# A decoder layer with expert retrieval: split weights in the first pass, selection in halves, w_o by blocks, plain fp32 for every other first-table tile

## The chip, the cores and the metric

One core of a Trainium2 chip. The metric is device time in microseconds for one execution of the program. The engines named below are TensorE (PE; its weight loads are PEld), VectorE (DVE), ScalarE (ACT), GpSimd (POOL, which issues the indirect gathers) and SyncE (SP, which issues nearly all other DMAs).

## The reference, cut to what matters

512 tokens, width 1024, all float32. One layer and a final norm:

```python
xn = rmsnorm(h, ln_mix_g)
q, k, v, pz, ga, gp = split(xn @ w_in + b_in)        # 30 column blocks of 128
y_a = sliding_window_attention(q, k, v, sinks) @ w_attn_up
y_p = multiscale_pool(pz, w_pool_grp, pool_scale) @ w_pool_up
h = h + (sigmoid(ga) * y_a + sigmoid(gp) * y_p) @ w_o
xn = rmsnorm(h, ln_ffn_g)
# retrieval: 8 heads, two halves of 128 keys each
sc = einsum(xn @ w_query, sub_keys)                  # 16 column blocks of 128
sv, si = top_k(sc, 16)                               # per token, head and half
fv, fi = top_k(all pairs of sv, 16); idx = pairs of si at fi   # 128 experts of 16384 per token
a = gelu(sum(u_tab[idx] * xn)); g = softmax(fv)      # per token and chosen expert
h = h + sum((g * a) * v_tab[idx])
out = rmsnorm(h, ln_final_g)
```

## The kernel before

**Tokens.** Four blocks of 128 tokens. The mixing runs in two passes of two blocks (`mixing`, L179): blocks 0 and 1 (GB, CB), then blocks 2 and 3. The retrieval is done in two ways. Blocks 2 and 3 go through the whole expert tables as matrix products ("dense"). Block 0 fetches its 128 u rows and 128 v rows per token by indirect DMA. Block 1 fetches its u rows only, and takes part in the dense product with the v table. One gathered row tile (128 tokens by 1024, 512 KB) with the DVE operation on it is called a unit: 128 dots for block 1, 128 dots and 128 additions for block 0, so 384 units in all.

**Products.** fp32 operands go to PE as they are (`mm`, L198, two instructions for each product). Split operands (`mm3`, L112) are high and low parts in the fp32r type, three instructions for each product; the high part is an ACT cast (L124), the low part a DVE subtraction (L119).

**A pass.** Normalise and transpose the inputs (`xT`), project k and v (z 8, 9), then q (z 0 to 7) with attention woven in, then four pooling columns (z 10 to 13), sixteen gate columns (z 14 to 29), the two up projections (L276), w_o for both blocks together (L293, eight weight tiles), residual and second norm, the turn of the normed rows into `qx` (L311), then the sixteen w_query columns with the match against the sub keys (`match`, L322) and the top 16 of each (`top16`, L479). All projections of both passes are plain fp32. A weight tile is 512 KB, in one of four raw buffers (`raw`, L130). The second pass is a generator that starts (inputs, k and v) before the first pass's w_query (`hooks[2]`).

**Selection.** `select` (L492) turns the top 16 of all heads of a block into 128 expert numbers (`ei`) and weights (`gw`), all on DVE but one exponential.

**Background work.** `feed` (L169) takes work from a list: selection of block 1, 40 dots of block 1, selection of block 0, the other 88 dots, then block 0's dots and additions. `tick` (L175) spends a given cost from that list at points of the second pass; what it traces is ordered behind the last "paced" instruction, but only on that instruction's engine. In most of the pass that is ACT, so DVE and POOL work may be issued earlier; in the up projections and in w_o it is a DVE instruction (L288). Within the mixing and table stages a greedy scheduler orders each engine's instructions by readiness and program order.

**First table stage** (`run`, L760). For each of the 128 u tiles, `part` loads it, splits it and makes 24 split products for blocks 2 and 3 (`u_part`, L605); the gelu goes to a held tile or to DRAM (`ahead`). Beside each tile 3.4 cost units of selection (blocks 2 and 3) and of one-hot work are spent (`onehot`, L548: three times, ACT makes 5 of 8 matrices in the first two), and 0.9 units of gathered rows.

**Dense stage** (`dense`, L684). Written out by hand: for each of the 128 v tiles a weight `mix`, the split of the v tile, 18 products of 128 x 512, and an equal share of the units that are left.

Of the kernel before, what the change touches and what calls it, by code (L numbers as in the profile page):

```python
# [11 lines left out]
F32 = mybir.dt.float32  # L12
# [7 lines left out]
P = 128  # L20
# [43 lines left out]
class Layer:  # L64
# [69 lines left out]

    def norm(self, x, g, out):
# [43 lines left out]
    def mixing(self, mp, b0, xn2, hooks):  # L179
# [4 lines left out]
        xT = self.m.tile([P, KD, TU], F32, name="xT", tag="xT", bufs=2)  # L184
# [15 lines left out]
        def z(f, dst, w=None):  # L200
            ps = self.mm_tile(TU)
            mm(ps, w or self.raw(a["w_in"][f]), xT)
# [8 lines left out]
        w89 = [None, None]  # L211
        if first:
            w89 = [self.raw(a["w_in"][f]) for f in (8, 9)]
            hooks[0]()
        for x, r in zip(xs, rows):
            n = t4()
            self.norm(x, self.gm, n)
            self.across(n, lambda ps, r=r: nc.scalar.copy(xT[:, :, r], ps))
        kz, vT = t2()[:, :TU], t2()[:, :TU]
        z(8, kz, w89[0])  # L220
# [4 lines left out]
        z(9, vT, w89[1])  # L225
# [50 lines left out]
        for h in range(4):  # L276
# [12 lines left out]
            tick(2.5 * T_O)  # L289
# [3 lines left out]
        ps = [self.big([P, 2, 512], "ho") for _ in bs]  # L293
        for k in range(KD):
            w = self.raw(a["w_o"][k])
            for j, r in enumerate(rows):
                for n in range(2):
                    nc.tensor.matmul(ps[j][:, n, :], lhsT=mT[:, k, r], rhs=w[:, n * 512:(n + 1) * 512],
                                     start=k == 0, stop=k == KD - 1)
            tick(T_W)  # L300
        hooks[2]()
        qx = self.m.tile([P, KD, TU], F32, name="xT", tag="xT", bufs=2)
        for j, b in enumerate(bs):
# [3 lines left out]
            nc.vector.tensor_tensor(hb, ps[j].rearrange("p a b -> p (a b)"), hb, op=ALU.add)  # L307
            if b != GB:
                nc.sync.dma_start(out=self.hspill[b - CB], in_=hb)
            nat = self.nat[b] if first else t4()  # L310
            self.norm(hb, self.gf, nat)  # L311
            puts = [lambda ps, r=rows[j]: nc.scalar.copy(qx[:, :, r], ps)]  # L312
            if not first:
                puts.append(lambda ps, r=rows[j]: self.low(ps, xn2[0][:, :, r], xn2[1][:, :, r]))
                puts.insert(1, lambda ps, r=rows[j]: nc.scalar.copy(xn2[0][:, :, r], ps))
            self.across(nat, *puts)
# [5 lines left out]
        def match(i, qT):  # L322
# [6 lines left out]
            for j, b in enumerate(bs):  # L329
# [6 lines left out]
        for i in range(16):  # L336
            w = self.raw(a["w_query"][i])
            ps = self.mm_tile(TU)
            mm(ps, w, qx)
# [5 lines left out]
            tick(T_S)  # L345
        match(i, last)

    def mixed(self, xn2):
        nc, a, tc = self.nc, self.a, self.tc
        with tc.tile_pool(name="merged", bufs=1) as self.m, ExitStack() as ps, tc.tile_pool(name="mixing", bufs=1) as mp:  # L350
# [14 lines left out]
            two = self.mixing(mp, HALF, xn2, (nothing, nothing, nothing))  # L365
            one = self.mixing(mp, 0, None, (rest, self.consts, lambda: next(two)))
            for _ in one:
                pass

            def room():  # L370
                t = mp.tile([P, 2048], F32, name="sk", tag="sk", bufs=1)
# [19 lines left out]
            def picked(b):  # L391
                yield from self.select(room(), eq, self.sv[b], self.si[b], self.ei[b], self.gw[b])
# [7 lines left out]
            assert self.work[2].done  # L400
# [91 lines left out]
    def select(self, t, wide, sv, si, ei, g):  # L492
# [3 lines left out]
        v.tensor_copy(sf, si)  # L496
        svp = sv.rearrange("p (h t) k -> p h t k", t=2)
        sfp = sf.rearrange("p (h t) k -> p h t k", t=2)
        v.tensor_scalar(sfp[:, :, 0, :], sfp[:, :, 0, :], float(NKEY), None, op0=ALU.mult)
        cv, ce = t("cv", [P, PH, NCAND]), t("ce", [P, PH, NCAND])  # L500
        for src, dst in ((svp, cv), (sfp, ce)):
            for a0, na, n, off in SEGS:
                v.tensor_tensor(dst[:, :, off:off + na * n].rearrange("p h (a b) -> p h a b", a=na),
                                src[:, :, 0, a0:a0 + na].unsqueeze(3).to_broadcast([P, PH, na, n]),
                                src[:, :, 1, :n].unsqueeze(2).to_broadcast([P, PH, na, n]), op=ALU.add)
        fv, fi = t("fv", [P, PH, TOPK]), t("fi", [P, PH, TOPK], U32)
        yield 5 * SC
        for n in range(0, PH, 4):
# [4 lines left out]
        v.tensor_copy(ff, fi)  # L513
        g = g.rearrange("p (h k) -> p h k", h=PH)
        v.tensor_tensor(g, fv, fv[:, :, 0:1].to_broadcast([P, PH, TOPK]), op=ALU.subtract)
        few = t("few", [P, PH, NFEW])
        for a0, na, n, off, at in FEW:
            v.tensor_copy(few[:, :, at:at + na * n], ce[:, :, off:off + na * n])
        for k0, k1, nh, pos, cand in ((0, 8, 4, self.fewpos, few), (8, 16, 2, self.iota[:, :NCAND], ce)):
            nk, w = k1 - k0, cand.shape[2]  # L520
            for h in range(0, PH, nh):
                if k0 == 8 and h == 0:
                    nc.scalar.activation(g, g, AF.Exp)
# [7 lines left out]
        v.tensor_copy(ei, ef.rearrange("p h k -> p (h k)"))  # L531
        den = t("gden", [P, PH])
        v.reduce_sum(den, g, axis=AX.X)
        v.reciprocal(den, den)
        v.tensor_tensor(g, g, den.unsqueeze(2).to_broadcast([P, PH, TOPK]), op=ALU.mult)
# [69 lines left out]
    def u_part(self, n, w, xn2):  # L605
# [290 lines left out]
```

## Time and profile before

| what | us |
|---|---|
| three runs | 1760.51, 1753.23, 1763.14 (median 1760.51) |
| profiled execution | 1754.47 |
| its span | 1752.7 |
| first pass, up to its last w_query column | about 0 to 303 |
| second pass, up to its last match | about 303 to 640 |
| first table stage | about 640 to 1166 |
| dense stage and end | about 1166 to 1753 |

Over the span PE is busy 1572.9 us (90%), DVE 1275.5 (73%), ACT 726.9 (41%), POOL 535.3 (31%); 486.34 MB are moved, 277 GB/s in the mean. A share of the whole span says little here, since the stages have different limits; the rows below are by stage. A matmul's duration is not its cost: products are pipelined, and the cost is the distance from one start to the next.

### The profile page before, as it was taken

To read this page: it belongs to the slowest core of one execution; us is meant where nothing else is said; L and a number is where in the kernel's file an instruction comes from. 1 tells how busy PE (TensorE), PEld (TensorE's weight loads), DVE (VectorE), ACT (ScalarE), POOL (GpSimd) and SP (SyncE) were. 2 spreads that over 40 slices of the span, in tenths; PEclk is the share of its full clock that TensorE was granted. 3 is DMA by queue.
4 is the path that set the end of the run, shared out by engine and by line. 5 is a ranking of instruction groups with operands and counts; after the bars stand their busy time and mean duration, and the time that the engine had idled before them with its cause. 6 is when DMAs were issued, how large, how long until landed. Compare 5 with 4: busy or idle time off the path is not lost.

```text
span 1752.7 us, 24708 instructions
## 1 busy us (share of the span) xinstructions
PE 1572.9 (90%) x8701; PEld 1346.2 (77%) x8701; DVE 1275.5 (73%) x2797; ACT 726.9 (41%) x1391; POOL 535.3 (31%) x390
## 2 busy tenths in 40 slices
PE   6999999578995978889999999989999999998997
PEld 5788678456872868878888999978778777777876
DVE  2520126898067579997787899759989888888988
ACT  3531021242201124479999766433333333333334
POOL 0000000056007202343222233325555555454551
PEclk9999999798997989989999999999999999999999
DMA  5344443179549637679999999998999999999995
GB/s 175 114 154 152 156 139 133 40 286 363 195 161 383 228 126 248 245 266 327 314 333 317 326 351 350 367 300 317 362 357 389 381 371 351 378 369 375 375 340 185
DMA packets 188027, 486.34 MB, mean 277 GB/s; under 512 B 17024, under 2 KB 82560, under 8 KB 184576
## 3 DMA queue, kind: packets, MB, share of 16 engines
q1 hardware_dynamic: 131392, 279.75, 45.6%
q0 software_dynamic: 55296, 201.35, 31.5%
q10 hardware_dynamic: 1216, 3.67, 0.6%
q8 instruction: 68, 1.11, 0.3%
q14 instruction: 55, 0.45, 0.1%
HBM read 447.35 MB, written 36.83 MB: 276 GB/s over the span
## 4 chain that ended last, share of the span: by engine, by line
PE 31%; ACT 10%; DMA 8%; DVE 6%; issue 3%; SPq 0%; DVEq 0%; ACTq 0%
DMA wr<-v_experts 7%; PE acc L115 6%; PE acc L116 6%; PE acc L114 6%; PE mm L114 4%; PE mm L116 3%; PE mm L115 3%; DVE wl L119 3%; ACT wh L124 3%; ACT gs L589 2%; PE pg L588 2%; ACT ohj L576 2%; ACT ohj L567 2%; DVE row L707 1%; DMA gar<-ahead 1%
## 5 line engine op out<-in xcount | busy, mean ns | idle before, releaser
L701 POOL DMA_INDIRECT row<-u_experts,ei x256 | 342.6, 1338 | 944.4 <-DVE row L707 406.0
L119 DVE TENSOR_TENSOR wl<-wr,wh 128x1024 fp32r<-128x1024 f32 x256 | 311.5, 1219 | 88.6 <-ACT wh L124 87.6
L124 ACT CAST wh<-wr 128x1024 fp32r<-128x1024 f32 x256 | 268.2, 1049 | 184.7 <-PE mm L115 120.6
L198 PE MATMUL mm<-xT,wr 128*128 128x256 f32 x1472 | 337.1, 387 | 3.3 <-ACT xT L312 2.2
L115 PE MATMUL acc<-wl,wh 128*128 128x512 f32 x768 | 305.9, 398 | 20.3 <-DVE wl L119 20.2
L114 PE MATMUL mm<-xh,wh 128*128 128x256 f32 x1024 | 296.2, 291 | 28.6 <-ACT gk L618 12.7
L707 DVE SCALAR_TENSOR_TENSOR row<-row,nat 128x1024 f32<-128x1024 f32 x256 | 309.6, 1217 | 15.4 <-DMA row<-u_experts,ei 15.0
L198 PEld LDWEIGHTS mm<-xT,wr 128*128 128x128 f32 x1472 | 282.1, 194 | 45.9 <-issue 3.4
L114 PE MATMUL acc<-wh 128*128 128x512 f32 x768 | 303.5, 395 | 14.7 <-ACT wh L124 7.7
L116 PE MATMUL acc<-wh,wl 128*128 128x512 f32 x768 | 302.5, 394 | 0.0
L116 PE MATMUL mm<-xh,wl 128*128 128x256 f32 x1024 | 288.4, 285 | 15.6 <-DVE wl L119 15.0
L115 PE MATMUL mm<-xl,wh 128*128 128x256 f32 x1024 | 288.7, 283 | 0.0
L701 POOL DMA_INDIRECT row<-v_experts,ei x128 | 192.0, 1500 | 235.2 <-DVE hg L730 180.0
L114 PEld LDWEIGHTS mm<-xh,wh 128*128 128x128 f32 x1024 | 193.8, 190 | 37.0 <-ACT gk L618 16.1
L116 PEld LDWEIGHTS mm<-xh,wl 128*128 128x128 f32 x1024 | 193.1, 190 | 19.1 <-DVE wl L119 19.1
L115 PEld LDWEIGHTS mm<-xl,wh 128*128 128x128 f32 x1024 | 194.4, 190 | 0.0
L115 PEld LDWEIGHTS acc<-wl,wh 128*128 128x128 f32 x768 | 146.3, 191 | 60.8 <-DVE wl L119 30.9
L114 PEld LDWEIGHTS acc<-wh 128*128 128x128 f32 x768 | 146.3, 191 | 50.2 <-ACT wh L124 11.4
L116 PEld LDWEIGHTS acc<-wh,wl 128*128 128x128 f32 x768 | 146.4, 191 | 29.7
L730 DVE SCALAR_TENSOR_TENSOR hg<-row,act,hg 128x1024 f32<-128x1024 f32 x128 | 163.6, 1278 | 0.5
L656 ACT CAST wh<-gt 128x128 fp32r<-128x128 f32 x128 | 38.1, 298 | 282.8 <-PE acc L115 236.6
L588 PE MATMUL pg<-ohi,ohj 128*128 128x128 f32 x768 | 103.0, 285 | 7.0 <-ACT ohj L576 6.6
(185 smaller groups left out, 1627.5 us busy)
## 6 DMA issues: line engine op xcount, KB each, us to landing
wr<-u_blocks SPq DMA_DIRECT2D x128, 512.0 KB
wr<-v_experts SPq DMA_DIRECT2D x128, 512.0 KB
wr<-w_in SPq DMA_DIRECT2D x60, 512.0 KB
spill<-gs SPq DMA_DIRECT2D x24, 1024.0 KB
gt<-spill SPq DMA_DIRECT2D x64, 384.0 KB
wr<-w_query SPq DMA_DIRECT2D x32, 512.0 KB
wr<-w_attn_up SPq DMA_DIRECT2D x16, 512.0 KB
wr<-w_o SPq DMA_DIRECT2D x16, 512.0 KB
```

Of the source, the lines that this page charges most:

```text
L114: mm(out, lhsT=l[0], rhs=r[0], start=first, stop=False)
L115: mm(out, lhsT=l[0], rhs=r[1], start=False, stop=False)
L116: mm(out, lhsT=l[1], rhs=r[0], start=False, stop=last)
L119: self.lowered = self.nc.vector.tensor_tensor(lo, src, hi.bitcast(F32), op=ALU.subtract).ins
L124: self.nc.scalar.copy(hi, raw)
L198: nc.tensor.matmul(ps, lhsT=w[:, k * P:(k + 1) * P], rhs=x[:, k, :], start=k == 0, stop=k == nk - 1)
L567: nc.scalar.activation(ohj[:, z, :], self.iota, AF.Abs, bias=tr[:, 1, u + z:u + z + 1])
L588: nc.tensor.matmul(pg[:, z, :], lhsT=ohj[:, z, :], rhs=ohi[:, z, :], start=True, stop=True)
L656: nc.scalar.copy(h1, g1)
L701: self.nc.gpsimd.indirect_dma_start(out=t, out_offset=None, in_=tab, in_offset=bass.IndirectOffsetOnAxis(ap=ei[:, s:s + 1], axis=0))
L707: self.nc.vector.scalar_tensor_tensor(u, u, 1.0, self.nat[b], op0=ALU.mult, op1=ALU.mult, accum_out=self.act[b][:, s:s + 1])
L730: nc.vector.scalar_tensor_tensor(z, v, self.act[GB][:, s:s + 1], z, op0=ALU.mult, op1=ALU.add)
```

## The change

1. **First pass in split products.** `plan` and `fetch` load, cast and subtract each w_in and w_query tile of the first pass, one tile ahead; high and low parts lie in the six row buffers that the gathers use later. `xh`, `xl` take the place of `xT` and `qx` there. The second pass stays plain fp32.
2. **w_o one block at a time**: eight weight tiles for block 0, residual and norm, the same eight again for block 1 (16 loads a pass). Then `turn(0)`, the start of the next pass, in the second pass the first halves of three w_query columns (`FILL`), `turn(1)`.
3. **Selection by halves of the heads.** Heads 0 to 3 of block 1 are selected inside the first pass's w_query (`hooks[3]`). In the second pass block 1's dots are woven with the rest of the selection (`weave`).
4. **Every other u tile plain**: odd tiles skip the split and use 8 fp32 products with `xf`, a third copy of the normed rows.
5. **Rates**: 1.2 units beside each u tile in place of 0.9; one-hot and selection work at 2.2, 3.6, 4.0 and 2.6 by stage, choose(3) woven with spread(2); ACT makes 6 of 8 one-hot matrices; 53 held tiles in place of 69. In the dense stage the two casts and two subtractions of `mix` become one of each.

```diff
-R_A = 3.4
-R_U = 0.9
-T_Z, T_A, T_O, T_W, T_S = 7.0, 2.0, 2.6, 2.5, 0.9
+R_U = 1.2
+T_Z, T_A, T_O, T_M, T_W, T_S = 4.0, 1.6, 2.7, 4.8, 1.35, 0.7
+LOOK = 1
+FILL = 3
-HELD = (46, 23)
+HELD = (39, 14)
-ZA = 5
+ZA = 6
+DOTS, PICKS = 1.1, 1.0
...
+    def fetch(self):
+        while self.planned and len(self.ready) <= LOOK:
+            raw = self.raw(self.planned.pop(0))
+            w = tuple(self.rows.tile([P, D], F32R, name="row", tag="row") for _ in "hl")
+            self.split(raw, *w)
+            self.ready.append(w)
+        return self.ready.pop(0)
...
+        def mmx(ps, src, x):
+            if not first:
+                return mm(ps, self.raw(src), x)
+            w = self.fetch()
+            for k in range(KD):
+                c = slice(k * P, (k + 1) * P)
+                self.mm3(ps, (w[0][:, c], w[1][:, c]), (xh[:, k, :], xl[:, k, :]), k == 0, k == KD - 1)
...
-            tick(2.5 * T_O)
+            tick(T_M)
...
-        ps = [self.big([P, 2, 512], "ho") for _ in bs]
-        for k in range(KD):
-            w = self.raw(a["w_o"][k])
-            for j, r in enumerate(rows):
+        for j, b in enumerate(bs):
+            ps = self.big([P, 2, 512], "ho")
+            for k in range(KD):
+                w = self.raw(a["w_o"][k])
...
+                tick(T_W)
...
+            nats.append(self.nat[b] if first else t4())
+            self.norm(hb, self.gf, nats[j])
...
+        turn(0)
+        hooks[2]()
+        early = {}
+        if not first:
+            for i in range(FILL):
+                w, ps = self.raw(a["w_query"][i]), self.mm_tile(TU)
+                early[i] = w, ps
+                for k in range(KD):
+                    nc.tensor.matmul(ps[:, :P], lhsT=w[:, k * P:(k + 1) * P], rhs=xf[:, k, :P], start=k == 0,
+                                     stop=k == KD - 1)
+        else:
+            self.plan([a["w_query"][i] for i in range(16)])
+        turn(1)
...
+            if i == 8:
+                hooks[3]()
...
-            self.near = Background(picked(CB))
-            self.dotted = [Background(self.dots(CB, 0, 40)), Background(self.dots(CB, 40, P))]
-            self.work = [self.near, self.dotted[0], Background(picked(GB)), self.dotted[1],
-                         Background(self.gather())]
+            def early():
+                for _ in picked(CB, 0, PH // 2):
+                    pass
...
+            def picks():
+                yield from picked(CB, PH // 2, PH)
+                self.chosen = True
+                yield from picked(GB, 0, PH)
...
+            self.dotted = Background(weave((rows(), DOTS), (picks(), PICKS)))
+            self.work = [self.dotted, Background(self.gather())]
...
+            if plain:
+                nc.tensor.matmul(ps, lhsT=w[:, c], rhs=xn2[2][:, k, :], start=k == 0, stop=k == KD - 1)
...
+            plain = ahead % 2 == 1
             with tc.high_priority(HP):
-                w = self.weights(a["u_blocks"][ahead])
-                after = self.lowered
-            self.u_part(ahead, w, xn2)
+                w = (self.raw if plain else self.weights)(a["u_blocks"][ahead])
+            after = self.u_part(ahead, w, xn2, plain)
...
-            bg = Background(choose(2), choose(3), spread(2), spread(3), spread(CB))
-            while not bg.done:
-                after = part()
-                with tc.issue_after(after):
-                    bg.spend(R_A)
-                    self.feed(R_U)
+            for steps, rate in ((choose(2), 2.2), (weave((spread(2), 2.4), (choose(3), 1.0)), 3.6), (spread(3), 4.0),
+                                (spread(CB), 2.6)):
+                bg = Background(steps)
+                while not bg.done:
+                    after = part()
+                    with tc.issue_after(after):
+                        bg.spend(rate)
+                        self.feed(R_U)
...
+def weave(*parts):
+    live = [[0.0, share, steps] for steps, share in parts]
+    while live:
+        p = min(live, key=lambda p: p[0] / p[1])
+        cost = next(p[2], None)
+        if cost is None:
+            live.remove(p)
+        else:
+            p[0] += cost
+            yield cost
```

## Rows read from the trace of the kernel before

**Rows 1.** The page's slices, 40 equal parts of the span, DMA share in tenths.

```profile
DMA  5344443179549637679999999998999999999995
```

**Rows 2.** Busy time by stretch; after DVE, ACT, POOL: clock, DMA share, GB/s.

```profile
27.00:96.00 69.00, 63.63 (x355) 49.28 (x354) 32.47 (x85) 34.63 (x109) 0.00 (x0) 1.00 0.39 129
...
336.00:426.00 90.00, 69.94 (x343) 53.74 (x344) 76.94 (x148) 29.37 (x83) 44.63 (x39) 0.88 0.72 263
...
517.00:572.00 55.00, 32.49 (x86) 15.99 (x85) 42.94 (x70) 7.42 (x11) 34.75 (x24) 0.80 0.91 350
...
757.00:1000.00 243.00, 218.25 (x1754) 211.70 (x1755) 196.36 (x328) 228.21 (x456) 70.03 (x54) 0.97 0.91 318
1000.00:1107.00 107.00, 105.46 (x892) 104.28 (x891) 105.86 (x196) 68.14 (x73) 37.88 (x26) 1.00 0.97 348
...
1200.00:1700.00 500.00, 472.03 (x2007) 379.18 (x2006) 444.24 (x724) 179.38 (x342) 266.38 (x183) 0.98 1.02 369
```

**Rows 3.** PE's waits, 240 to 350 and 540 to 650: total us, times, longest.

```profile
PE pt L439 <- DVE den L431: 20.0, 1, 20.0
...
PE tr L148 <- DVE t L143: 21.4, 2, 13.1
PE mm L116 <- DVE wl L119: 8.7, 1, 8.7
```

**Rows 4.** Timeline, PE: start us, us, instructions (plain, split, dense products).

```profile
308.88 7.17 PE L198 MATMUL mm<-xT,wr 128*128 128x256 f32 x32
...
1060.12 0.28 PE L114 MATMUL mm<-xh,wh 128*128 128x256 f32 x1
...
1060.48 0.28 PE L114 MATMUL mm<-xh,wh 128*128 128x256 f32 x1
...
1210.50 0.39 PE L114 MATMUL acc<-wh 128*128 128x512 f32 x1
...
1211.18 0.39 PE L114 MATMUL acc<-wh 128*128 128x512 f32 x1
```

**Rows 5.** Timeline, DVE, end of the first pass: top 16, then selection of block 1.

```profile
301.04 0.87 DVE L482 MAX8 sv<-t 128x8 f32<-128x128 f32 x4 [3.03 <-ACT t L331]
...
310.41 0.27 DVE L503 TENSOR_TENSOR sk<-sv 128x128 f32<-128x128 f32 x1
...
335.94 0.28 DVE L535 TENSOR_TENSOR gw<-gw,sk 128x128 f32<-128x128 f32 x1
```

**Rows 6.** The chain that ended last, in order: start us, us, what.

```profile
739.08 1.14 DVE wl L119
740.22 1.14 DVE row L707 x2
...
1456.78 15.06 DMA wr<-v_experts
```

**Rows 7.** Gathers by stretch: POOL busy and count, clock, DMA share, GB/s.

```profile
0.00:640.00 640.00, 96.09 (x76) 0.94 0.54 189
640.00:1166.00 526.00, 156.48 (x114) 0.97 0.87 307
1166.00:1753.00 587.00, 282.03 (x194) 0.98 0.97 347
```

**Rows 8.** Gelus of the u tiles by stretch: ACT busy and count (table loads included).

```profile
652.00:757.00 105.00, 14.98 (x33) 0.98 0.72 246
757.00:1000.00 243.00, 19.68 (x51) 0.97 0.91 318
1000.00:1107.00 107.00, 10.12 (x28) 1.00 0.97 348
1107.00:1166.00 59.00, 7.11 (x20) 1.00 0.94 348
```

**Rows 9.** ACT's groups from 757 to 1000.

```profile
L589 ACT COPY gs<-pg 128x1024 f32<-128x1024 f32 x32 | 63.3, 1984 | 0.0
L124 ACT CAST wh<-wr 128x1024 fp32r<-128x1024 f32 x52 | 54.5, 1051 | 15.1 <-PE mm L115 14.8
```

More of the change, by code (lines that the diff above doesn't have):

```diff
@@ L133, in raw, with plan @@
         return w
+    def plan(self, srcs):
+        self.planned, self.ready = list(srcs), []
+    def fetch(self):
[5 more added lines that the diff above has]
+        return self.ready.pop(0)
     def norm(self, x, g, out):
@@ L183, in mixing @@
         rows = [slice(j * P, (j + 1) * P) for j in range(HALF)]
-        xT = self.m.tile([P, KD, TU], F32, name="xT", tag="xT", bufs=2)
+        xh, xl, xf = xn2
+        xT = None if first else self.m.tile([P, KD, TU], F32, name="xT", tag="xT", bufs=1)
         def t2():
@@ L210, in mixing @@
                 nc.scalar.dma_start(out=self.gm, in_=a["ln_mix_g"][0].partition_broadcast(P))
-        w89 = [None, None]
         if first:
-            w89 = [self.raw(a["w_in"][f]) for f in (8, 9)]
+            self.plan([a["w_in"][f] for f in (8, 9, *range(8), *range(10, 30))])
+            self.ready.insert(0, self.fetch())
             hooks[0]()
@@ L217, in mixing @@
             self.norm(x, self.gm, n)
-            self.across(n, lambda ps, r=r: nc.scalar.copy(xT[:, :, r], ps))
+            self.across(n, *(pair(r) if first else whole(xT, r)))
         kz, vT = t2()[:, :TU], t2()[:, :TU]
-        z(8, kz, w89[0])
+        z(8, kz)
         cols = slice(b0 * P, (b0 + HALF) * P)
@@ L306, in mixing, with turn @@
                 nc.sync.dma_start(out=hb, in_=a["x"][0, b * P:(b + 1) * P, :])
-            nc.vector.tensor_tensor(hb, ps[j].rearrange("p a b -> p (a b)"), hb, op=ALU.add)
+            nc.vector.tensor_tensor(hb, ps.rearrange("p a b -> p (a b)"), hb, op=ALU.add)
             if b != GB:
                 nc.sync.dma_start(out=self.hspill[b - CB], in_=hb)
[L310 to L316, printed above, removed]
+            nats.append(self.nat[b] if first else t4())
+            self.norm(hb, self.gf, nats[j])
+        def turn(j):
+            r = rows[j]
+            self.across(nats[j], *(pair(r) if first else whole(xf, r) + pair(r)))
+        turn(0)
[11 more added lines that the diff above has]
+        turn(1)
         subk = mp.tile([P, 16, P], F32, name="sk", tag="sk", bufs=1)
@@ L336, in mixing @@
         for i in range(16):
-            w = self.raw(a["w_query"][i])
-            ps = self.mm_tile(TU)
-            mm(ps, w, qx)
+            if i in early:
+                w, ps = early.pop(i)
+                for k in range(KD):
+                    nc.tensor.matmul(ps[:, P:], lhsT=w[:, k * P:(k + 1) * P], rhs=xf[:, k, P:], start=k == 0,
+                                     stop=k == KD - 1)
+            else:
+                ps = self.mm_tile(TU)
+                mmx(ps, a["w_query"][i], xf)
             qT = t2()[:, :TU]
@@ L363, in rest @@
                 nc.sync.dma_start(out=self.mask, in_=a["mask"])
[L365 to L368, printed above, removed]
             def room():
-                t = mp.tile([P, 2048], F32, name="sk", tag="sk", bufs=1)
+                t = mp.tile([P, 2048], F32, name="rm", tag="rm", bufs=1)
                 at = 0
@@ L389, in eq, with picked, rows @@
                 return v.rearrange("p (a b c) -> p a b c", a=shape[1], b=shape[2])
-            def picked(b):
-                yield from self.select(room(), eq, self.sv[b], self.si[b], self.ei[b], self.gw[b])
-            self.near = Background(picked(CB))
-            self.dotted = [Background(self.dots(CB, 0, 40)), Background(self.dots(CB, 40, P))]
-            self.work = [self.near, self.dotted[0], Background(picked(GB)), self.dotted[1],
-                         Background(self.gather())]
+            def picked(b, h0, h1):
+                return self.select(room(), eq, self.sv[b], self.si[b], self.ei[b], self.gw[b], h0, h1)
+            def early():
+                for _ in picked(CB, 0, PH // 2):
+                    pass
+            two = self.mixing(mp, HALF, xn2, (nothing, nothing, nothing, nothing))
+            for _ in self.mixing(mp, 0, xn2, (rest, self.consts, lambda: next(two), early)):
+                pass
+            def picks():
+                yield from picked(CB, PH // 2, PH)
+                self.chosen = True
+                yield from picked(GB, 0, PH)
+            def rows():
+                yield from self.dots(CB, 0, P // 2)
+                assert self.chosen
+                yield from self.dots(CB, P // 2, P)
+            self.chosen = False
+            self.dotted = Background(weave((rows(), DOTS), (picks(), PICKS)))
+            self.work = [self.dotted, Background(self.gather())]
             for _ in two:
                 pass
-            assert self.work[2].done
+            print("before tables", self.units)
     def attention(self, t4, b, quad, q, tq, kT, vn, put):
@@ L603, in onehot, with u_part @@
         product(n, *last)
-    def u_part(self, n, w, xn2):
+    def u_part(self, n, w, xn2, plain):
         nc = self.nc
@@ L762, in run @@
         self.units = 3 * PH * TOPK
-        xn2 = tuple(self.x.tile([P, KD, TU], F32R, name="x" + n) for n in "hl")
+        xn2 = tuple(self.x.tile([P, KD, TU], F32 if n == "f" else F32R, name="x" + n) for n in "hlf")
         self.mixed(xn2)
@@ L796, in spread @@
                 if b == CB:
-                    while not self.dotted[1].done:
+                    while not self.dotted.done:
                         self.feed(1)
```

87 lines of the change are left out of this document (46 added, 41 removed).

## Prediction

> **What bounds the kernel now.** I read the page's slices first, then busy time by stretch, since no share of the whole span says which limit holds where. The slices show the transfers below half in the first pass and nearly full from the table stage on [rows 1]; the stretches show four different limits [rows 2]. In the second pass's attention (336 to 426) DVE is busy 77 of 90 us and PE 70; PE has no long product there that it could not have done sooner. Around w_o and the second norm (517 to 572) PE works 32 of 55 us. In the table stage ACT is full from 757 to 1000 (228 of 243), then PE and DVE both to 1107. In the dense stage the transfers are full at 369 GB/s, with PE at 94% and DVE at 89%. PE's waits name the places between the stages: 20.0 us until DVE had the first softmax of the second pass, 21.4 us for the second norm, 8.7 us for the first low part of a u tile [rows 3]. The chain ends in the dense stage with steps such as one v load of 15.06 us [rows 6], so a byte taken out of that stage is worth time, until PE binds.
>
> **The prices.** The distance between starts counts. Two plain tiles (32 instructions) take 7.07 us but for the last product's tail, 3.43 us a tile; three split products start 0.36 us apart (1060.12 to 1060.48), 24 take 2.86 us; three dense products take 0.68 us, the 18 of a v tile 4.08 us [rows 4]. A low part and a dot take DVE 1.14 us each [rows 6], a cast takes ACT 1.05 [rows 9]. The top 16 of two blocks' four columns take 9.4 us (301.04 to 310.41), one block's selection about 25 us (310.41 to 336, with two softmaxes between) [rows 5].
>
> A split tile thus saves 0.57 us of PE against a plain one. The Trainium skill (FP8 and Floating Point Precision, TensorE Precision Notes) says that true FP32 makes four passes through the array; against three single passes that would be 0.86 us a tile, 9 us more saved in the first pass's z columns and 18 us more lost in the tables. The trace shows 1.20 between the two kinds, not 1.33, and the measurement decides. Every other number here goes by the rows' 0.57.
>
> **Part by part**, against the profiled execution (span 1752.7, own time 1754.5).
>
> *First pass to w_query.* 30 z columns save 30 x 0.57 = 17 us of PE. The price is 30 x 1.14 of DVE and 30 x 1.05 of ACT; from 27 to 96 both are half free (32 and 35 of 69 us) [rows 2], so they fit, but 14 columns lie between softmax steps where PE follows DVE; I count half of their 8 us. The first cast and subtraction add 1.5 us at the start. w_o by blocks leaves PE's work as it is, doubles 8 loads (16 x 0.52 MB in 27 us, 310 GB/s, with no gathers beside them: it fits), and lays block 0's norm beside block 1's products: 2 us. So w_query starts 13 us earlier, at about 224 in place of 237.
>
> *First w_query.* PE would need 16 x 2.86 plus the match. But DVE must now do 16 low parts (18), top 16 (4 x 9.4 = 38) and half a selection (13), 69 us, and is idle for some 7 us at the start. In program order a low part stands behind the top 16 traced before it, so PE follows DVE and the 9 us of 16 x 0.57 are not gained. DVE is through at 224 + 76 = 300, in place of 310 before the whole selection. The other half is woven in later, so the first softmax of the second pass is ready at about 312 in place of 336 [rows 3, 5]: **24 us**, the 13 included.
>
> *Second pass to the gates.* The gathers of heads 0 to 3 can begin near 295, not 359. DVE's load between first softmax and gates is 77 us now; after it is softmax and pooling (some 34) plus what is traced there: 32 cost units, 17 dots (19 us) and 15 of selection (10 us), and what is pulled forward. PE's stalls there shrink a little: **4 us** (bounds 8 lost, 15 gained).
>
> *w_o and the turn.* Now 27 us of products and 28 of waiting and transposes. Of the waiting, block 0's norm goes beside products, and three half columns (3 x 1.7 us) fill block 1's. Against that, 16 loads in 27 us meet some 15 gathers, 16 MB, at the 350 GB/s of that stretch now [rows 2] 46 us for w_o and the turn together; and in SP's queue block 0's residual load and store (L306, L309) stand among block 1's loads, the store waiting for DVE's addition (L307), which stands behind dots. I take **0** (bounds 12 either way), and **5 us** for the half columns in w_query.
>
> *Entry to the tables.* The 8.7 us for the first low part [rows 3] are filled by odd tiles, which need none: 5 us, in the next sum.
>
> *Table stage.* By the credits the stage falls into 19 tiles with choose(2), 38 with spread(2) and choose(3), 24 with spread(3), 37 with spread(CB), 10 alone. Per tile, PE needs (2.86 + 3.43) / 2 = 3.15 plus 0.30 for each one-hot unit (16 x 16 instructions over 94.5 units, at no more than the split product's 0.12 us); DVE 0.57 + 1.2 x 1.14 + its share; ACT 0.52 + 0.4 plus 0.97 a unit (now (228 - 55 - 20) = 153 us for 32 groups [rows 2, 8, 9], 63 of them the copy L589, so 0.57 a matrix and a sixth matrix more); transfers 0.52 + 1.2 x 0.52 MB plus spills, at 357 GB/s. The limit is DVE at 3.6, then PE and transfers at 4.05, ACT at 4.85, transfers at 4.3, and 3.3: 68 + 154 + 116 + 159 + 33 = 530 us. The same reckoning for the kernel before gives 515, where the rows have 514 for 128 tiles (30, 51, 28 and 20, the first count with three table loads) [rows 8]. So 15 us more, less the 5 of the entry, and less some because tiles are issued where engines are free (as in 652 to 757): **8 us lost** (bounds 18 gained, 38 lost). It buys 38 units: 154 in place of 114.
>
> *Dense stage.* Following the ticks, 70 units are done before the tables now and 184 after them (76 and 190 gathers issued, six buffers ahead [rows 7]); after the change 69 and 222. The dense stage has 162 left, not 200: 1.33 a tile for 1.64. Bytes per tile: 0.52 (v) + 0.20 (gates) + 0.07 to 0.08 (reloads, 14 more in all) + units x 0.52, from 1.64 MB to 1.50. At 369 GB/s that is 4.44 us before (the rows have some 4.41, 565 us for 128) and 4.06 after, below PE's 4.08. With both near full I take 4.18: **30 us gained** (bounds 17 and 42, the last PE alone). DVE falls to 3.7 us a tile.
>
> **Sum.** 24 + 4 + 0 + 5 - 8 + 30 = 55 us: 1754.5 - 55 = 1699.5. The median of the three runs lies 6 us above the profiled execution, so 1705 for the median.
>
> **The rivals.** (a) *The front gives nothing*: DVE's order in the first w_query (bursts of 9.4 us and the half selection ahead of low parts) and w_o's doubled loads eat the 33 us. For it: PE's largest waits are all on DVE there. Against: DVE's sum is smaller until the first softmax. 1738. (b) *The tables are dearer*: PE's 36 us (64 x 0.57) and the transfers of 38 units come in full, tables +38: 1735. For it: 0.97 of the transfers are used from 1000 on [rows 2]. (c) *The tables cost less*: ACT's and DVE's relief in 652 to 1000 is worth 18 us: 1679. (d) *Front and tables both disappoint*: 1768, no change. (e) *Slower*: plain tiles hold one of four raw buffers until PE has finished with them, some 6 us where split tiles hold theirs 3 to 4. If loads take L, 128 tiles take 128 x (L + 6) / 4; at the 14 to 15 us of the full dense stage [rows 6] that is 640 us or more for the tables, 100 over my 534, and 1805 in all. It decides from L = 12.5. Against it: with 0.97 of the transfers in use the loads came in time from 1000 to 1107, PE busy 105 of 107 us [rows 2]. That the change doesn't do what it says (gathers not earlier, since the rows' buffers hold the last split weights) is inside (a).
>
> **Numbers.** Forecast 0.50 (1680 to 1722), (a) 0.18, (b) 0.12, (c) 0.09, (d) 0.06, (e) 0.05. Half a per cent, 9 us, is what a measurement of this kernel can tell from no change. Faster: forecast, (a), (b), (c), 0.89; same: (d), 0.06; slower: (e), 0.05. The range is 1660 to 1745, past (a) and (b) above and past (c) below; 0.11 lies above it, a few hundredths below.
>
> **What would show it.** Right: w_query of the first pass starting near 224 with DVE full in it; the first gather near 295; the second pass over near 605; a table stage of about 530 us with some 154 gathers; a dense stage with some 160 gathers and PE above 96%. Wrong: long PE waits on low parts (L119) in the first w_query beyond 20 us; w_o's products in the second pass stretched beyond 45 us; ACT or PE idle behind u loads in the tables; a dense stage still at 4.4 us a tile, which would mean that bytes were not its limit.

## The result, and the profile after

The changed kernel takes 1846.32 us (median of four runs, 1845.82 to 1856.58), the kernel before 1760.37 beside it: ratio 1.0509, 95% interval 1.0461 to 1.0556. It is 86 us slower, where 55 us faster was forecast. The profiled execution took 1846.02 us, its span is 1844.2.

The time by stage, cut at PE's last match of the second pass and its first product of the dense stage (starts in the two timelines; differences taken before rounding):

| stage | before | after | difference | forecast |
|---|---|---|---|---|
| both passes, to the last match | 637 | 643 | +6 | -33 |
| first table stage | 536 | 651 | +115 | +8 |
| dense stage to the end | 580 | 550 | -29 | -30 |

One of three sums held. The page's slices show the transfers, nearly full in the tables before [rows 1], uneven there now (the 15th to the 28th of forty):

```profile
DMA  5253743774489558878879877888899999999994
```

So does busy time by stretch (us; then busy us and instructions of PE, PEld, DVE, ACT, POOL; granted clock, DMA share, GB/s), to be read against [rows 2]:

```profile
347.00:435.00 88.00, 71.11 (x326) 53.22 (x327) 79.38 (x222) 28.45 (x81) 43.18 (x31) 0.83 0.75 256
531.00:585.00 54.00, 40.75 (x130) 19.66 (x128) 38.68 (x58) 7.10 (x11) 25.45 (x18) 0.94 0.97 368
660.00:760.00 100.00, 88.05 (x511) 79.08 (x510) 85.68 (x259) 35.38 (x70) 34.64 (x30) 0.95 0.83 288
760.00:1000.00 240.00, 202.29 (x1273) 185.16 (x1272) 150.09 (x245) 172.76 (x369) 73.42 (x57) 0.94 0.82 288
1000.00:1285.00 285.00, 238.83 (x1507) 219.19 (x1507) 170.06 (x289) 119.50 (x195) 76.26 (x62) 0.93 0.82 289
1300.00:1800.00 500.00, 490.60 (x2136) 401.93 (x2135) 426.92 (x587) 199.20 (x362) 195.29 (x155) 0.99 0.98 349
```

In the tables nothing is full any more. ACT fell from 228 of 243 us to 173 of 240, the transfers from 0.91 and 0.97 to 0.82, PE to 84%. A stage in which every engine and the transfers have room, and which is 115 us longer, points to engines and loads that wait for each other in a circle. The Trainium skill (Trainium Kernel Development and Optimization, Best Practices) says that consistent bubbles can mean that on-chip memory ran out. The trace agrees: what ran out here is the four raw buffers, and the casts waited 171.7 us for loads. ACT's waits from 660 to 1285 (total us, times, longest) begin with one that the kernel before does not have:

```profile
ACT wh L126 <- DMA wr<-u_blocks: 171.7, 47, 10.6
ACT gk L683 <- PE mm L675: 50.1, 15, 5.6
```

The casts' group from 760 to 1000 has the same releaser (what ended its waits), where [rows 9] has PE:

```profile
L126 ACT CAST wh<-wr 128x1024 fp32r<-128x1024 f32 x22 | 23.0, 1044 | 43.1 <-DMA wr<-u_blocks 43.1
```

And the chain that ended last (start us, us, what), which in the dense stage goes through v loads as it did [rows 6], goes through u loads in the tables now:

```profile
1219.59 8.18 DMA wr<-u_blocks
...
1263.39 5.83 DMA wr<-u_blocks
...
1738.42 11.65 DMA wr<-v_experts
```

Of the 64 casts that are left, 47 waited for their load. In the kernel before the same line waited 120.6 us in its table stage for PE to give back a split buffer, and never for a load: the loads were early. How the circle runs, by rows of the timeline (start us, us, engine, line, instruction, wait); at each SP row (SPq) two loads are issued, a plain tile's and then the next split tile's:

```profile
1180.29 0.81 SPq L134 DMA_DIRECT2D wr<-u_blocks  x2
...
1185.68 1.05 ACT L126 CAST wh<-wr 128x1024 fp32r<-128x1024 f32 x1 [6.12 <-DMA wr<-u_blocks]
...
1186.76 1.22 DVE L121 TENSOR_TENSOR wl<-wr,wh 128x1024 fp32r<-128x1024 f32 x1 [4.17 <-ACT wh L126]
...
1188.01 0.84 SPq L134 DMA_DIRECT2D wr<-u_blocks  x2
...
1193.95 1.05 ACT L126 CAST wh<-wr 128x1024 fp32r<-128x1024 f32 x1 [4.38 <-DMA wr<-u_blocks]
...
1195.03 1.23 DVE L121 TENSOR_TENSOR wl<-wr,wh 128x1024 fp32r<-128x1024 f32 x1 [0.32 <-ACT wh L126]
...
1196.29 0.81 SPq L134 DMA_DIRECT2D wr<-u_blocks  x2
...
1199.70 3.72 PE L675 MATMUL mm<-xf,wr 128*128 128x256 f32 x16 [1.73 <-ACT ga L683]
```

Issue at 1180.29, cast at 1185.68, subtraction done at 1187.98, and only then, at 1188.01, the next pair of loads. The plain tile whose load was issued at 1180.29 is used by PE at 1199.70 and gives its buffer back at 1203.4, 23 us after the issue. PE's waits before plain tiles close the circle. It waits for gelus (78 us, 29 waits over 0.3 us), and for 44 us of these the gelu stood on ACT right behind a cast that had waited for its load. The largest sum and one such case (PE's wait; then ACT's rows, and the chain):

```profile
PE mm L675 <- ACT ga L683: 56.7, 21, 12.5
...
1212.99 1.04 ACT L126 CAST wh<-wr 128x1024 fp32r<-128x1024 f32 x1 [5.97 <-DMA wr<-u_blocks]
1213.94 0.38 ACT L683 ACTIVATE ga<-mm 128x256 f32<-128x256 f32 x1
...
1214.37 5.20 PE mm L675 x16
```

PE's plain tile ends at 1219.57, and the load of 1219.59 in the chain above is the next. Followed through the whole stage in the same way (SP's issue, ACT's cast, the end of DVE's subtraction, PE's sixteen plain products; means over tiles 4 to 127, 62 split and 62 plain, worked out from those rows):

| us | before, split | after, split | after, plain |
|---|---|---|---|
| issue to first reader | 13.4 | 6.0 | 25.4 |
| raw buffer held | 16.1 | 8.8 | 29.5 |
| a tile | 4.05 | 4.98 | 4.98 |

There is one plain and one split tile per 9.96 us, so plain tiles hold 29.5 / 9.96 = 2.96 of the four raw buffers and split tiles 0.89. In the mean three of four buffers keep tiles for which PE is not ready; through the fourth goes one split tile at a time: load 6.0, cast and subtraction 2.8, then the next.

PE's waits from 215 to 350, against [rows 3]:

```profile
PE pt L497 <- DVE den L489: 13.5, 1, 13.5
PE mm L116 <- ACT row L111: 12.0, 2, 11.8
PE tr L161 <- DVE t L156: 8.0, 2, 7.4
PE mm L118 <- DVE row L121: 6.4, 3, 2.7
```

The 20.0 us before the first softmax became 13.5, but 26 us of new waits stand ahead of it, and it comes at 347.3 in place of 336. The gathers by stretch (POOL's busy us and count) went about as forecast, 38 units out of the dense stage [rows 7]:

```profile
0.00:650.00 650.00, 102.67 (x80) 0.94 0.59 202
650.00:1285.00 635.00, 185.41 (x148) 0.93 0.81 286
1285.00:1844.00 559.00, 197.15 (x156) 0.98 0.95 333
```

### The profile page after: what moved, and what is told of

It is laid out like the page before. It is cut to its first block, busy times and chain, and to the rows that moved or that the text cites. A ratio compares the mean times of both kernels' runs of the same rounds, so it can differ in the third digit from the quotient of the medians.

```text
span 1844.2 us, 24437 instructions
## 1 busy us (share of the span) xinstructions
PE 1610.5 (87%) x8605; PEld 1373.5 (74%) x8605; DVE 1257.2 (68%) x2653; ACT 738.3 (40%) x1436; POOL 485.9 (26%) x390
## 5 line engine op out<-in xcount | busy, mean ns | idle before, releaser
L121 DVE TENSOR_TENSOR wl<-wr,wh 128x1024 fp32r<-128x1024 f32 x192 | 234.8, 1223 | 145.8 <-ACT wh L126 143.2
L675 PE MATMUL mm<-xf,wr 128*128 128x256 f32 x1024 | 262.0, 414 | 78.4 <-ACT ga L683 56.7
L675 PEld LDWEIGHTS mm<-xf,wr 128*128 128x128 f32 x1024 | 207.7, 208 | 117.9 <-ACT ga L683 61.6
L126 ACT CAST wh<-wr 128x1024 fp32r<-128x1024 f32 x192 | 200.8, 1046 | 202.4 <-DMA wr<-u_blocks 183.1
L723 ACT CAST wh<-wf 128x384 fp32r<-128x384 f32 x128 | 65.7, 514 | 318.2 <-PE acc L117 255.5
L116 PE MATMUL mm<-xh,wh 128*128 128x256 f32 x512 | 152.7, 298 | 13.9 <-ACT gk L683 6.8
L118 PE MATMUL mm<-xh,wl 128*128 128x256 f32 x512 | 147.3, 288 | 7.7 <-DVE wl L121 7.7
L117 PE MATMUL mm<-xl,wh 128*128 128x256 f32 x512 | 149.0, 291 | 0.0
L116 PE MATMUL mm<-xh,row 128*128 128x256 f32 x368 | 109.6, 298 | 13.1 <-ACT row L111 12.0
L118 PE MATMUL mm<-xh,row 128*128 128x256 f32 x368 | 107.4, 292 | 6.4 <-DVE row L121 6.4
L116 PEld LDWEIGHTS mm<-xh,wh 128*128 128x128 f32 x512 | 98.1, 192 | 16.3 <-ACT gk L683 7.8
```

Source lines behind the costliest of these rows:

```text
L116: mm(out, lhsT=l[0], rhs=r[0], start=first, stop=False)
L117: mm(out, lhsT=l[0], rhs=r[1], start=False, stop=False)
L118: mm(out, lhsT=l[1], rhs=r[0], start=False, stop=last)
L121: self.lowered = self.nc.vector.tensor_tensor(lo, src, hi.bitcast(F32), op=ALU.subtract).ins
L126: self.nc.scalar.copy(hi, raw)
L675: nc.tensor.matmul(ps, lhsT=w[:, c], rhs=xn2[2][:, k, :], start=k == 0, stop=k == KD - 1)
```

## Experiments

Each is told with its profiled execution cut at the same two points; its medians stand beside those of the kernel before on the same chip. Two theories stood against each other for the tables: raw buffers that plain tiles hold, and the price of plain products on PE (64 x 0.57 = 36 us); a third was the order of the background work behind a plain tile's gelu.

### All u tiles split

```diff
-            plain = ahead % 2 == 1
+            plain = False
```

> The changed kernel with every u tile in split products again (only that part undone). It took 1844 us with a table stage of some 635 us (650 to 1285), 109 more than before. Theory T1, plain tiles hold one of the four raw buffers until PE is done with them, so loads start late and ACT waits for u loads (172 us in the stage): the stage falls to about 535, the whole to about 1745. Rival T2, the plain products' own price (64 x 0.57 = 36 us of PE) and the 34 more gathers: only 36 us come back, 1808. Rival T3, ACT's one-hot work is queued behind the gelu of a plain tile: as T1, 1745.

1747.20 us, ratio 0.9911 (0.9877 to 0.9944). Stages 641, 558, 550. Undoing one of the five parts turns 86 us slower into some 16 faster (by the ratio), and all but 2 us of the difference of the two profiled executions lie in the table stage (651 to 558). ACT waits for PE again, not for loads:

```profile
ACT wh L126 <- PE mm L117: 122.2, 59, 11.9
```

### Three buffers of their own for plain tiles

```diff
-HELD = (39, 14)
+HELD = (27, 14)
...
-                w = (self.raw if plain else self.weights)(a["u_blocks"][ahead])
+                w = (self.own if plain else self.weights)(a["u_blocks"][ahead])
```

`own` is `raw` with a tag "wp" of three buffers; the memory comes from 12 held tiles.

> The changed kernel, odd tiles still plain, but loaded into three buffers of their own, so that the four raw buffers serve split tiles alone (12 held tiles fewer to make room, 12 more stores and reloads of 128 KB). T1: loads can start early again, the table stage falls from 635 to 545 to 570, the whole to 1755 to 1780. T2 and T3: unchanged within 15 us, some 1844, or 5 us more for the reloads.

1777.06 us, ratio 1.0069 (1.0030 to 1.0109). Stages 643, 583, 549. Plain tiles stay plain and 69 us are gone; no wait of ACT on a u load is left. So most of the loss was the buffers and not the products. The edit does two things, seven buffers in place of four and a set of their own for plain tiles; seven shared buffers were not tried, so the two are not separated. The 25 us over the all-split table stage looked like PE's price of plain products. They were not, as the two runs below show.

### Background work behind the subtraction

```diff
-            return after if plain else self.lowered
+            return self.lowered
```

> The changed kernel, but the background work beside a plain tile is queued behind the last low part on DVE, as beside a split tile, not behind the plain tile's gelu on ACT. T3: ACT is free to run ahead, the table stage falls to about 545, the whole to 1755. T1 and T2: unchanged within 15 us of 1844.

1819.35 us (two runs), ratio 1.0317 (1.0161 to 1.0472). Stages 640, 622, 545. Worth 27 us on the medians, but the two runs lie 22 us apart and the interval meets that of the changed kernel, so how much it is worth here stays open. It is far from the 1755 of the third theory: ACT still waits for u loads (155.2 us of such waits), so the circle is the same.

### Both edits

> The changed kernel with both edits of the two runs before it: plain tiles in three buffers of their own (53 held tiles become 41), and the background work of every tile ordered behind the DVE subtraction. Apart they took 69 and 27 us off 1846. Theory: with own buffers the loads come early, and all that is left over the all-split kernel's 1747 is PE's price of 64 plain tiles, 64 x 0.57 = 36 us; the order then adds nothing: 1770 to 1785, u products over by about 1224. Rival: the two edits mend different waits and add up: 1750, table stage about 555 us.

1734.36 us (two runs), ratio 0.9820 (0.9743 to 0.9897). Stages 644, 539, 551. Below both expectations: with own buffers the order is worth 43 us, not nothing, and on the medians the kernel is 13 us faster than with all tiles split, though the intervals of the ratios overlap. The table stage now costs 3 us more than before and does 39 more units, where the prediction had 8 us more for 38. PE's price of plain products shows and is covered: against all tiles split PE is busy 506 us for 484 in the stage, ACT 333 for 395, DVE 425 for 498. That this relief is what shortens the stage is the reading here; no run takes it away by itself. The two table stages, own buffers alone (its worst part, and whole) and both edits:

```profile
760.00:1000.00 240.00, 194.17 (x1237) 180.43 (x1236) 144.84 (x225) 169.57 (x364) 74.22 (x53) 0.91 0.82 293
645.00:1215.00 570.00, 507.89 (x3290) 471.67 (x3291) 417.83 (x870) 329.96 (x633) 198.26 (x148) 0.95 0.88 323
```

```profile
645.00:1173.00 528.00, 497.33 (x3290) 462.15 (x3291) 424.54 (x887) 331.07 (x634) 211.72 (x153) 0.99 0.96 354
```

What the order did is in DVE's waits. With own buffers alone:

```profile
DVE row L776 <- DMA row<-u_experts,ei: 97.5, 27, 6.8
DVE wl L122 <- ACT wh L127: 33.1, 16, 4.6
```

With both edits:

```profile
DVE wl L122 <- ACT wh L127: 79.0, 38, 6.3
DVE ohj L641 <- PE pg L656: 7.5, 8, 2.0
```

Behind a plain tile's gelu, an ACT instruction, dots are not ordered on DVE at all. They went into its queue before their rows had been gathered, and DVE stood 97.5 us in front of them with the next tile's subtraction behind: from cast to the end of the subtraction it took 5.9 us in the mean, and 2.7 with both edits. Ordered behind a DVE instruction they waited 0.3 us for a gather in the whole stage.

### First pass in plain fp32

With all tiles split, the first pass loads its w_in and w_query tiles as before and `xf` holds its inputs; `plan` and `fetch` are not used.

```diff
-            if not first:
-                return mm(ps, self.raw(src), x)
...
+            return mm(ps, w or self.raw(src), x)
...
-            self.across(n, *(pair(r) if first else whole(xT, r)))
+            self.across(n, *whole(xT, r))
```

> The all-split kernel of e1 (1747 us) with the first pass in plain fp32 again; all else as changed. The first softmax product of the second pass came 11 us later than before (347 to 336) although the first pass's columns are shorter on PE. Theory F1, the low parts (46 x 1.14 = 52 us of DVE) delay DVE where PE waits for it, above all beside the top 16 in w_query: undoing the split costs nothing or gains, 1735 to 1750, with that product at 335 to 345. Rival F2, the split is worth its PE time (46 x 0.57 = 26 us) and something else lost it: the time rises to about 1770.

1741.60 us (two runs), ratio 0.9881 (0.9783 to 0.9979). Stages 634, 559, 549. The front is 8 us shorter than with the split, the medians 6 apart, no more than can be told from nothing. No gain from the split of the first pass shows.

### w_o for both blocks together

With all tiles split, each weight tile of w_o is loaded once a pass and used for both blocks.

```diff
+        pss = [self.big([P, 2, 512], "ho") for _ in bs]
+        for k in range(KD):
+            w = self.raw(a["w_o"][k])
+            for j, r in enumerate(rows):
...
         for j, b in enumerate(bs):
-            ps = self.big([P, 2, 512], "ho")
-            for k in range(KD):
-                w = self.raw(a["w_o"][k])
```

> The all-split kernel of e1 (1747 us) with w_o for both blocks together again (8 loads a pass). Theory W1, the 8 more loads a pass and the order of the turn cost what the hidden norm gains: within 8 us of 1747, the second pass's w_o to w_query some 54 us either way. Rival W2, the doubled loads cost more: w_o's products, stretched from 27 to some 45 us by waits for loads, return to 27, and the time falls by 10 to 15. Rival W3, the hidden norm was a gain: the time rises by 10 to 20.

1754.03 us, ratio 0.9932 (0.9899 to 0.9965); the front ends at 644, 3 us later. Seven us on the medians, but the intervals of the ratios overlap: the two orders of w_o can't be told apart, as W1 has it.

### No early selection

With all tiles split, block 1's whole selection goes back to the head of the background list.

```diff
-                for _ in picked(CB, 0, PH // 2):
-                    pass
+                pass
...
+            self.near = Background(picked(CB, 0, PH))
...
-            self.work = [self.dotted, Background(self.gather())]
+            self.work = [self.near, self.dotted, Background(self.gather())]
```

> The all-split kernel of e1 (1747 us) without the selection of four heads inside the first w_query: all of block 1 is selected at the start of the second pass, then the weave of its dots with block 0's selection. F1 (DVE order): PE's wait of 11.8 us in the first w_query goes, w_query ends some 12 us sooner, but the first softmax stands behind 13 us more of selection; in all within 8 us of 1747, the first gather at about 350 in place of some 310. Rival F3, the early half is worth its 13 us and 40 us of earlier gathers: 1760 or more.

1751.06 us, ratio 0.9920 (0.9888 to 0.9952). Stages of the profiled execution, its fastest: 615, 561, 564. The early selection costs the front 26 us (641 to 615), 17 of them ahead of the first softmax, and 14 come back in the dense stage (550 to 564), since 75 gathers were issued before the tables with it and 55 without. The time is the same within 4 us, but for the opposite of the reason forecast.

### Front edits together, and the rate alone

First, with all tiles split, the first pass in plain fp32 and no early selection together:

> All u tiles split, first pass in plain fp32, no early selection of heads 0 to 3 (the whole selection of block 1 stands first in the background list). Apart, these two moved the start of the u loads from 628 to 621 and to 603. If the early selection stood between DVE and the first softmax of the second pass, and the split was paid on DVE too, both shorten the front: u loads from about 596, some 14 us given back in the dense stage for units not done before: 1728 to 1736. Rival: both parts take the same waits of DVE away, and the front is no shorter than without the early selection alone: 1740 to 1745.

1740.86 us, ratio 0.9871 (0.9807 to 0.9935). Stages 614, 561, 564. Without the early selection the plain first pass adds nothing to the front (614 for 615): the first expectation missed, the rival's time came. On the medians it is 10 us below the run without the early selection alone, with intervals that overlap.

Then one number changed in the kernel before:

```diff
-R_U = 0.9
+R_U = 1.2
```

> The kernel before with one number changed: 1.2 units beside each u tile in place of 0.9 (some 38 more of the 384 units in the table stage). The dense term of the prediction by itself. Theory (bytes were the dense stage's limit): dense stage from 587 to about 559 us; the table stage longer by up to 30 us, by 18 as the all-split kernel had it (544 against 526): 1745 to 1757. Rival: a unit costs the same in either stage: 1760 within 5.

1749.31 us, ratio 0.9915 (0.9888 to 0.9943). Stages 638, 560, 549. The rate alone, in the kernel before, brings 13 us: the dense stage is 30 us shorter, the tables 24 longer. That is as much as all parts but the plain tiles bring together (ratio 0.9911 with all tiles split, 0.9915 here): the others gain nothing that can be told. Its table and dense stage:

```profile
640.00:1192.00 552.00, 482.70 (x3849) 467.73 (x3849) 505.07 (x979) 370.66 (x636) 221.19 (x153) 0.96 0.90 330
1192.00:1747.00 555.00, 529.17 (x2304) 432.48 (x2304) 471.00 (x770) 209.24 (x409) 206.87 (x155) 0.99 0.93 330
```

Last, the kernel with the two front edits (the first of this section) at a lower rate:

```diff
-R_U = 1.2
+R_U = 1.05
```

> The second kernel of this call with 1.05 units beside each u tile in place of 1.2, so 19 fewer in the tables and 19 more in the dense stage. By the dense term (30 us for 38 units) 15 us longer there, by the all-split table stage (18 us for 38) 9 us shorter in the tables: 6 us above that kernel. Rival: the tables are full of transfers in their middle, so a unit costs as much there: within 3 us of it, or below.

1744.91 us, ratio 0.9884 (0.9824 to 0.9944). Stages 616, 542, 581. Against that kernel 19 units less in the tables, 19 us less there and 17 more in the dense stage: where all tiles are split, a unit beyond 1.05 a tile costs about the same in either stage.

### The best of these

> Own buffers for plain tiles and the background behind the subtraction (1734 together), with the first pass in plain fp32 and without the early selection. With all tiles split the same two front edits moved the u loads from 628 to 602, and the kernel only from 1747 to 1741, since 14 units fewer were done before the tables. If those units cost their price in the dense stage only (PE full there), the mends and the front edits add up: 1734 - 6 = 1728. Rival: in the mended table stage (transfers 0.97, PE 224 of 240 us) the units that come from the front stand in the way: 1734 or above.

1720.95 us (1717.27 to 1724.79), ratio 0.9763 (0.9726 to 0.9801). Stages 612, 541, 563.

> The two mends with the first pass in plain fp32 alone, the early selection kept. With all tiles split the plain first pass was worth 6 us (1747 to 1742; u loads at 621 for 628). Theory: the split of the first pass is worth nothing and costs some DVE and ACT: 1727 to 1732. Rival: the 6 us were within what can be told apart: 1734 to 1738.

1722.99 us (1716.25 to 1727.96), ratio 0.9755 (0.9716 to 0.9794). Stages 634, 540, 552.

Both beat both kernels, by some 44 and 125 us, and can't be told apart. Both came in a little below their expectations; the 14 units of the first one were 20 gathers (75 and 55). In their profiled executions (1717.27 and 1727.96) the front is 22 us shorter without the early selection, and 11 of it come back in the dense stage. Against both edits with the split first pass, the plain one is 11 us faster on the medians; the intervals of the ratios overlap, but the front is 10 us shorter (634 for 644), as it was 8 with all tiles split. The table and dense stage of the first:

```profile
612.00:1153.00 541.00, 507.30 (x3339) 470.33 (x3339) 425.29 (x899) 334.20 (x642) 206.54 (x153) 0.99 0.96 351
1153.00:1715.00 562.00, 530.21 (x2304) 430.37 (x2302) 482.19 (x672) 220.19 (x407) 242.70 (x176) 0.99 0.96 346
```

## Why the prediction was wrong

**The table stage, "8 us lost (bounds 18 gained, 38 lost)": this step failed**, by over 100 us. The sum took the largest of each resource's work per tile. As a sum it came out once buffers and order were mended: 539 us beside 536, +3 for +8; the prices in it were not measured one by one. What it left out is that a tile occupies a buffer between its load and its last reader, which the run with own buffers priced at 69 us, and that work ordered on one engine is free on another, 43 us more. The bounds came from the prices and so could not hold this.

**Rival (e) named the mechanism and mis-sized it**, with 0.05. It had plain tiles hold a buffer some 6 us beyond the load, and loads of 14 to 15 us: 640 us for the tables (635 measured from 650 to 1285), 1805 in all. The agreement is luck, since the numbers behind it are others: the load of a split tile took 6.0 us, a plain tile was held 29.5, so some 23 beyond a load and not 6 (an estimate, with the same 6.0 for its load), and "decides from L = 12.5" was void. Put into the rival's own form, the measured holds give 64 x (29.5 + 8.8) / 4 = 613 us. The 6 us counted one tile's products. But PE takes tiles in order, and three pairs of high and low parts let loads run far ahead of it; a split tile waits for PE in those, a plain one in the raw buffer. That distance can be read in the kernel before, from one tile's load, cast and first product:

```profile
1042.12 0.33 SPq L132 DMA_DIRECT2D wr<-u_blocks  x1
...
1054.99 1.05 ACT L124 CAST wh<-wr 128x1024 fp32r<-128x1024 f32 x1 [3.08 <-PE mm L115]
...
1062.98 0.37 PE L114 MATMUL mm<-xh,wh 128*128 128x256 f32 x1
```

From issue to first product 20.9 us, 21.9 in the mean of 124 tiles; with 3.7 of plain products a plain tile would hold its buffer 25.6, an estimate. Half the tiles at 25.6 and half at 16.1 make 128 x 20.85 / 4 = 667 us of four buffers, an alarm of 130 us that stood in the trace. The argument put against (e), that loads came in time from 1000 to 1107 with the transfers at 0.97, was about a kernel in which every tile leaves the raw buffer at the subtraction.

**The first softmax, "24 us": failed**, at +11 (347.3 for 336.1). Two parts. w_query was to start at 224 and did at 240.2, where the kernel before has 237.3: w_o began 5 us sooner, but in the turn PE waits 7.4 us for a norm of the second pass's inputs. The split is not the reason: with the first pass in plain fp32 the same wait is 6.4 us and w_query starts at 239.8. What both have is the new order: in the kernel before, the start of the next pass stands ahead of the residuals in the program, and DVE made these two norms at 93.7 and 95.3, inside the first pass; now it stands behind them, and the norms come at 225.3 and 227.8, after block 1's residual and norm. The prediction had no term for that. No run puts it back alone, so this cause is read from the timelines and not shown. Then the sum of 69 us took DVE to work through. It did not, as the timeline of the first w_query shows, with DVE's idle time in brackets:

```profile
244.26 1.23 DVE L121 TENSOR_TENSOR row<-wr,row 128x1024 fp32r<-128x1024 f32 x1 [3.40 <-ACT row L111]
247.14 1.23 DVE L121 TENSOR_TENSOR row<-wr,row 128x1024 fp32r<-128x1024 f32 x1 [1.65 <-ACT row L111]
250.46 1.23 DVE L121 TENSOR_TENSOR row<-wr,row 128x1024 fp32r<-128x1024 f32 x1 [2.09 <-ACT row L111]
253.77 1.23 DVE L121 TENSOR_TENSOR row<-wr,row 128x1024 fp32r<-128x1024 f32 x1 [2.09 <-ACT row L111]
...
283.25 0.21 DVE L556 CAST rm<-si 128x128 f32<-128x128 uint32 x1
```

While PE has the rows' buffers full DVE waits for it; when the half selection starts at 283.25 it holds PE's next weights until 294.4, a PE wait of 11.8 us: ACT's cast of them stands behind an exponential and a copy that wait for the selection on DVE (5.0 and 4.0 us). With all tiles split the same softmax came at 347.3, without the early selection at 330.6, with the first pass plain at 338.6, with both at 328.1: the early selection costs 10 to 17 us there, the split 2 to 9. A half selection moved from behind the top 16 into the columns is not saved: it stands there at its price, in front of the weights, and what it brings is gathers from 305 on rather than 359.

**"4 us" to the gates, "0" for w_o, "5 us" for the half columns**: from the first softmax to the last match 295 us in place of 301, 5 for 9. w_o's products in the second pass were spread over 44 us, just under the 45 that the prediction gave as a sign, and from the start of w_o to the first match it took 57.6 us in place of 63.6; together with the run that joins the blocks again (3 us in the front) these small terms are right within their bounds.

**The dense stage, "30 us gained": right**, 29 measured, 156 gathers for some 160, PE 98% busy for "above 96%". The rate alone gave 30 in the kernel before, so the term has the right cause, the units that leave the stage. A unit takes DVE time as well as bytes, and no run separates them; for bytes speak the transfers, 1.02 before with PE at 94% and DVE at 89% [rows 2].

**The sign.** Five of the six cases, 0.95 of the chance, took the table stage to lie within 38 us of before.

## What to carry to other kernels

Before an operation is moved off a copy and onto the buffer that was loaded, read in the trace how far its reader stands behind the load (issue to first use), multiply by the tiles per microsecond, and compare with the number of buffers: here 29.5 us at one plain tile per 10 us wanted three buffers of four, and three more buffers brought 69 us. A sum of work by engine is a lower bound and says nothing of such a circle; its mark in the profile is a stage in which nothing is full and a load's first reader waits for the load. And an ordering "behind instruction X" in an in-order queue protects only the engine of X: work for another engine goes in early and blocks that one.

## What was not expected of the hardware

Idle time of PE cost twice here. After a wait of 5.19 us in the tables a plain tile took 5.50 us in place of 3.72, and its first part ran at a granted clock of 0.50 (the lower level, 1.2 GHz). The timeline row, and the two stretches (wait, then products):

```profile
1179.61 5.50 PE L675 MATMUL mm<-xf,wr 128*128 128x256 f32 x16 [5.19 <-ACT ga L683]
```

```profile
1174.40:1179.60 5.20, 0.02 (x1) 0.00 (x0) 0.57 (x1) 1.60 (x3) 0.00 (x0) 0.69 0.92 368
1179.60:1182.00 2.40, 2.39 (x6) 1.94 (x7) 2.40 (x3) 0.00 (x0) 0.00 (x0) 0.50 0.33 67
```

Over the table stage the granted clock was 0.93 in the changed kernel and 0.99 with both edits, and a plain tile's sixteen products took 4.11 us and 3.69 in the mean of 62 tiles. And with the transfers at 0.82, split tiles were read 6.0 us after the issue of their load, in the mean; the 14 to 15 us taken for a load were those of the full dense stage.
